# Grouped-query attention on one core: where VectorE computes the first step of its exponential correction, and when Q is transposed

## The chip, the core and the metric

The kernel runs on one core of a Trainium2 chip. Its engines are TensorE (PE in the profile; PEld is its weight load), VectorE (DVE), ScalarE (ACT), GpSimd (POOL) and SyncE (SP, which issues transfers here). The metric is the device time of one execution in microseconds (us); several executions are made and their median is compared.

## What is computed

```python
batch, seq, n_heads, n_kv_heads, dim = 8, 512, 32, 8, 64
K_expanded = np.repeat(K, heads_per_group, axis=2)      # heads_per_group = 4
V_expanded = np.repeat(V, heads_per_group, axis=2)
scores = np.einsum('bhqd,bhkd->bhqk', Q, K_expanded) * scale      # scale = 1/sqrt(dim)
weights = np.exp(scores - np.max(scores, axis=-1, keepdims=True))
weights = weights / (np.sum(weights, axis=-1, keepdims=True) + 1e-10)
output = np.einsum('bhqk,bhkd->bhqd', weights, V_expanded)
```

All inputs and the output are float32.

## The kernel before

The kernel takes the exponential without subtracting the maximum, and checks at the end whether the sums and V lay in bounds in which that is safe; if not, a second, general path computes everything again. Only the first path matters here.

The work is cut into 64 jobs. A job is one key/value head of one batch entry, with its four query heads. Two jobs make a unit `u` (a pair of key/value heads), so `u, g = divmod(j, 2)`. For each job TensorE computes the scores transposed (keys on the partitions, queries along the row), 16 blocks of 128 keys by 512 queries (four heads by four chunks of keys); each block is exponentiated into the tile `pt`; then TensorE multiplies `pt` with V, to which a column of ones is added, so that the product `pv` holds the outputs and the sums; VectorE takes the reciprocal of the sums (`inv`) and multiplies (`o_sb`), in two halves per job (`norm(j, 0)` and `norm(j, 1)`).

The exponentials are dealt to two routes:

- ScalarE does most: tiles of two blocks (128x1024, from an `s_ps` buffer, of which there are two) with an Exp activation (`act_tile`, L301). A job has seven of them, `act_tile(j, 0)` to `act_tile(j, 6)`.
- VectorE and GpSimd do the rest, `taken(j)` blocks of a job: two in a narrow job, three in a wide one. `WIDE(j)` holds for jobs from 4 on whose number isn't divisible by three, so a round of three jobs is narrow, wide, wide (called here the first and the second wide job). In a wide job `act_tile(j, 4)` is a half tile (128x512), which lies in one bank of `d_ps`.

The route of VectorE and GpSimd for the taken blocks has these steps: scores into `d_ps`; `u`, an affine map of the scores to 16-bit integers (VectorE, L312; two blocks at the job's start, and the third of a wide job already at the end of the job before); `f`, the low ten bits of u (VectorE, L323, the "and-step"); `g`, an affine map of f, the first step of the correction (GpSimd, L326); `w`, the product of g and f (GpSimd, L330); and `pt = u + w` (VectorE, L339, `exp_d4`, the "add"). The add of a job is done in the job after.

The products with V read the blocks of the upper half in the order 2, 3, 1, 0 of the key chunks, since VectorE's blocks lie in chunks 0 and 1; products from the 17th on need the add.

Q is loaded as it lies and transposed by TensorE against an identity, eight transposes a job (`trans_q`, L215) into one bank of `d_ps`, from which VectorE copies it to `qt` (L220). `d_ps` is one buffer of two banks, `pv` is one buffer of two banks, `s_ps` two buffers of two banks.

The order on each engine is the order in which the program issues its instructions, so each engine runs its own part of the loop body strictly in turn and waits where it needs another's result. In the middle of a job the order in the program is: the first half's normalization `norm(last, 0)`, tile 3, a new `d_ps` tile, tile 4 if the job is wide, the Q transposes of job j + 2, the check of sums (`check_sums`, L378, two VectorE instructions once in eight jobs, only in narrow jobs), the and-step, g and w of this job, the add of the last job, the copy of Q, tile 4 if the job is narrow, and then the products of the last job's second half, cut in three by `cut` with tiles 5 and 6 between, and the third block of the next job (`exp_d(j + 1, 2, ...)`) if that is wide.

The Tile layer adds the waits from what the instructions read and write. `apart` declares that two instructions don't depend on each other, where they touch different banks of one tile.

Of the kernel before, what the change touches and what calls it, by code (L numbers as in the profile page):

```python
# [40 lines left out]
WIDE = lambda j: j >= 4 and j % 3 > 0  # L41
# [26 lines left out]
def fast_path(ctx, tc, Q, K, V, out, flag, ident):  # L68
    nc = tc.nc
# [77 lines left out]
    def d_tile():  # L147
        return d_pool.tile([128, 2, S], FP32, name="d_ps")
# [3 lines left out]
    def first_k(gp, swap, bank):  # L152
        half_bank = bank.bitcast(BF16)[:, 0:S]
        ps = half_bank.rearrange("p (sc c) -> p sc c", sc=SC)
        h = 2 * gp
        done = []
        for sc in range(SC):
            if swap:
                for half, g in ((0, 1), (64, 0)):
                    done.append(nc.tensor.transpose(  # L160
                        ps[half:half + 64, sc, :], kn[0][:, sc, h + g, :], ident
                    ))
            else:
                done.append(nc.tensor.transpose(ps[:, sc, :], kn[0][:, sc, h:h + 2, :], ident))
        return done, lambda: nc.vector.tensor_copy(
            out=kt_first[:, gp, swap, :], in_=half_bank
        )
# [32 lines left out]
    def apart(this, other):  # L200
        if other is not None:
            tc.declare_no_dep(
                this.ins, other.ins, reason="the two are in different banks of one tile"
            )
        return this

    def trans_q(j, bank, lo=0, hi=NPAIR, other=None):
        u, g = divmod(j, 2)
        ps = bank.bitcast(BF16).rearrange("p (i sc c) -> p i sc c", i=NPAIR, sc=SC)
        done = []  # L210
        for i in range(lo, hi):
            for sc in range(SC):
                h = (u % 2) * 2 * HPG + g * HPG + 2 * i
                done.append(apart(
                    nc.tensor.transpose(ps[:, i, sc, :], qn[u // 2][:, sc, h:h + 2, :], ident),  # L215
                    other,
                ))
        if u not in qt:
            qt[u] = qt_pool.tile([128, 2, NPAIR, S], BF16, name="qt")
        return done, lambda: apart(nc.vector.tensor_copy(  # L220
            out=qt[u][:, g, lo:hi, :], in_=ps[:, lo:hi, :, :].rearrange("p i sc c -> p i (sc c)")
        ), other)
# [20 lines left out]
    NJOB = NU * 2  # L243
    DPAIR = NPAIR - 1

    def taken(j):
        return 1 if j == NJOB - 1 else 3 if WIDE(j) else 2

    def d_block(j):
        return SC * 2 - 2 if j == NJOB - 1 else 0  # L250

    def act_tiles(j):
        every = [(i, kc, m) for i in range(NPAIR) for kc in range(SC) for m in range(2)]
        first = DPAIR * SC * 2 + d_block(j)
        mine = [n for n in range(len(every)) if not first <= n < first + taken(j)]
        groups = [[n for n in mine if n // 2 == h] for h in range(len(every) // 2)]
        return [[every[n] for n in group] for group in groups if group]

    jobs, osb, invs = {}, {}, {}

    CHECKS = {}
    for b in range(B):
# [32 lines left out]
    def act_tile(j, n, spare=None):  # L295
        group = act_tiles(j)[n]
        i, kc, lo = group[0]
        ps = s_pool.tile([128, 2, S], FP32, name="s_ps") if spare is None else spare
        for _, _, m in group:
            scores(j, ps[:, m, :], i, kc, m)  # L300
        return nc.scalar.activation(  # L301
            out=jobs[j]["pt"][:, i, kc, lo:, :], in_=ps[:, lo:, :], func=EXP, scale=scale
        )

    def exp_d(j, lo, hi, ps, other=None):
        st = jobs.setdefault(j, {})
        if "u" not in st:
            for name, dtype in (("u", I16), ("f", I16), ("g", BF16), ("w", BF16)):
                st[name] = dve_pool.tile([128, 3, S], dtype, name=name + "16")[:, 0:taken(j), :]
        for n in range(lo, hi):  # L310
            apart(scores(j, ps[:, n - lo, :], DPAIR, *divmod(d_block(j) + n, 2)), other)
        return lambda: nc.vector.tensor_scalar(  # L312
            out=st["u"][:, lo:hi, :], in0=ps[:, 0:hi - lo, :], scalar1=A_U, scalar2=B_U,
            op0=ALU.mult, op1=ALU.add,
        )
# [3 lines left out]
    def exp_d2(j, engine=None):  # L319
        st = jobs[j]  # L320
        by_bits = engine is None
        engine = engine or nc.gpsimd
        nc.vector.tensor_single_scalar(  # L323
            out=st["f"], in_=st["u"], scalar=1023, op=ALU.bitwise_and
        )
        engine.tensor_scalar(  # L326
            out=st["g"], in0=st["f"], scalar1=-EXP_F1, scalar2=EXP_K * 2.0 ** (24 * by_bits),
            op0=ALU.add, op1=ALU.mult,
        )
        product = lambda: engine.tensor_tensor(  # L330
            out=st["w"], in0=st["g"], in1=st["f"].bitcast(FP16) if by_bits else st["f"],
            op=ALU.mult,
        )
        return product() if by_bits else product

    def exp_d4(j):
        st = jobs[j]
        n = taken(j)
        nc.vector.tensor_tensor(  # L339
            out=st["pt"][:, DPAIR, :, :, :].rearrange("p kc m q -> p (kc m) q")[  # L340
                :, d_block(j):d_block(j) + n, :
            ].bitcast(U16),
            in0=st["u"],
            in1=st["w"],
            op=ALU.add,
        )
# [8 lines left out]
    def pv(j, i, lo, hi):  # L355
        st = jobs[j]
        u, g = divmod(j, 2)
        b, gp = divmod(u, GP)
        if lo == 0:

            t = d_tile() if (j, i) == (NJOB - 1, 0) else pv_tile()
            t = t.rearrange("p m (qc c) -> p m qc c", qc=SC)
            st["pv"][i] = t[:, :, :, 0:D + 1]
        order = blocks(j, i)
        for n in range(lo, hi):
            kc, m, qc = order[n]
            nc.tensor.matmul(  # L367
                st["pv"][i][:, m, qc, :],
                st["pt"][:, i, kc, m, qc * 128:(qc + 1) * 128],
                vt[b % 2][:, kc, 2 * gp + g, :],  # L370
                start=(n < 2 * SC and qc == 0),
                stop=(n >= len(order) - 2 * SC and qc == SC - 1),
            )
# [139 lines left out]
    bank = pv_tile()  # L513
# [41 lines left out]
    bank = pv_tile()  # L555
# [7 lines left out]
    for j in range(1, NJOB - 1):  # L563
        last = j - 1
        u, g = divmod(j, 2)
        b, gp = divmod(u, GP)
        open_job(j)
        if j == 1:
            nc.gpsimd.tensor_copy(out=gate, in_=jobs[0]["pt"][0:1, 0, SC - 1, 0, 0:1])
        for load, *of in LOADS.get(j, ()):  # L570
            load(*of)
        if j == 1:
            dma_k(0, 2)
        if gp == 2 and g == 0 and b + 1 < B:
            dma_k(b + 1)

        cut = (11, 19) if taken(j) < 3 else (4, 18) if taken(last) < 3 else (4, 16)
        act_tile(j, 0)
        if j == 1:
            piece(1, *first_k(1, 0, bank[:, 1, S // 2:]))  # L580
        exp_d(j, 0, 2, d_tile())()
        act_tile(j, 1)
        if (j, 0) in CHECKS:
            check_v(*CHECKS[j, 0])
        pv(last, 0, 0, 16)
        act_tile(j, 2)
        pv(last, 0, 16, 32)
        norm(last, 0)
        act_tile(j, 3)

        reads = []
        bank = d_tile()
        beside = act_tile(j, 4, bank) if taken(j) > 2 else None

        ahead = (j + 1,) if j < 2 else (3, 4) if j == 2 else (j + 2,)
        for n, to in enumerate(ahead):
            if to < NJOB:
                reads.append(trans_q(to, bank[:, n, :], other=beside)[1])
        if j == 1:
            reads.append(first_k(1, 1, bank[:, 1, :])[1])  # L600
        if not WIDE(j):
            check_sums()
        exp_d2(j)
        exp_d4(last)
        copies = [read() for read in reads]
        if taken(j) == 2:
            act_tile(j, 4)
        pv(last, 1, 0, cut[0])
        act_tile(j, 5)
        if beside:  # L610
            pv(last, 1, *cut)
        if taken(j + 1) > 2:
            exp_d(j + 1, 2, taken(j + 1), bank[:, 1:2, :], copies[0])()
        if (j, 1) in CHECKS:
            check_v(*CHECKS[j, 1])
        if not beside:
            pv(last, 1, *cut)
        act_tile(j, 6)
        pv(last, 1, cut[1], 32)
        norm(last, 1)  # L620
        del jobs[last]

    j, last = NJOB - 1, NJOB - 2
# [144 lines left out]
```

## Time and profile before

| | |
|---|---|
| runs | 408.16, 408.46, 414.83 us; median 408.46 |
| profiled execution | 408.25 us; span of its instructions 406.5 us |
| mean granted TensorE clock | 0.999 |
| TensorE busy | 376.4 us, 93% of the span |
| VectorE busy | 353.0 us, 87% |
| ScalarE busy | 397.3 us, 98% |
| GpSimd busy | 328.2 us, 81% |
| g on GpSimd, 128x1536 | x40, mean 1971 ns |
| w on GpSimd, 128x1536 | x40, mean 3094 ns |
| Q copy on VectorE | x62, mean 682 ns |
| add on VectorE, 128x1536 | x40, mean 951 ns |

The table is read from the first and the fifth part of the page and from the groups by shape. Busy times are of the union of an engine's instructions, so where instructions of one engine overlap (ScalarE's do), the mean of one times their number is more than the busy time. A share of 100% isn't needed for an engine to set the time, and idle time of an engine that doesn't set it costs nothing. In rows of groups the columns are line, engine, operation, output and inputs with their shapes, count, busy time and mean ns of one, and idle time in front with what ended it. In rows of the timeline they are start, length, engine, line, operation, tiles, shapes, count of merged instructions and, in brackets, the idle time in front.

### The profile page before, as it was taken

What the parts mean: (1) busy time and instruction counts of PE and PEld (TensorE: products, weight loads), DVE (VectorE), ACT (ScalarE), POOL (GpSimd) and SP (SyncE); (2) the same over time, 40 slices, a digit from 0 to 9 for tenths busy, and PEclk for the clock granted to TensorE, in tenths of its full rate; (3) what the DMA queues carried; (4) which work ended last, traced back from release to release, by engine and by line L of the source; (5) the groups of instructions that cost most, each with busy time, mean ns of one, the idle gap of its engine ahead of it and who ended that gap; (6) DMA issues with size and microseconds to landing.
All of it is one profiled execution on the core that took longest, in us unless ns stands there. A gap on an engine that the chain in (4) does not pass through costs nothing.

```text
span 406.5 us, 12968 instructions
## 1 busy us (share of the span) xinstructions
PE 376.4 (93%) x5670; PEld 231.9 (57%) x5670; DVE 353.0 (87%) x618; ACT 397.3 (98%) x455; POOL 328.2 (81%) x181
## 2 busy tenths in 40 slices
PE   7999999999999999999999999999999999989985
PEld 3565565565555555655555555655565555655643
DVE  4788998988898989999889989889888999899875
ACT  5999999999999999999999999999999999999995
POOL 9978878878779879788888888788887798677682
PEclk9999999999999999999999999999999999999999
DMA  9999999977587996889497999949797496222205
GB/s 145 162 242 151 196 262 271 224 195 154 119 199 150 99 223 168 194 162 204 125 233 52 188 218 228 147 174 147 187 226 207 137 98 141 106 105 105 105 21 192
DMA packets 82892, 67.72 MB, mean 167 GB/s; under 512 B 52752, under 2 KB 57872, under 8 KB 82832
## 3 DMA queue, kind: packets, MB, share of 16 engines
q0 software_dynamic: 45072, 24.91, 52.0%
q1 hardware_dynamic: 37216, 41.75, 36.3%
q8 instruction: 45, 0.74, 0.8%
q10 hardware_dynamic: 544, 0.20, 0.2%
q14 instruction: 15, 0.12, 0.1%
HBM read 50.33 MB, written 33.55 MB: 206 GB/s over the span
## 4 chain that ended last, share of the span: by engine, by line
ACT 75%; PE 19%; DVE 3%; issue 1%; ACTq 0%; DVEq 0%
ACT pt L301 75%; PE s_ps L283 9%; PE pv L367 7%; PE d_ps L283 2%; DVE o_sb L414 1%; PE s_ps L503 1%; PE d_ps L215 1%; DVE u L312 0%; DVE pt L339 0%; ACT pt L535 0%; ACTq L301 0%; DVE inv_last L409 0%; PE d_ps L367 0%; DVE okv L238 0%; DVE ok L378 0%
## 5 line engine op out<-in xcount | busy, mean ns | idle before, releaser
L301 ACT ACTIVATE pt<-s_ps 128x1024 f16<-128x1024 f32 x408 | 385.7, 1179 | 0.5 <-PE s_ps L283 0.4
L367 PEld LDWEIGHTS <-pt 128*128 128x128 f16 x4096 | 142.6, 98 | 79.0 <-issue 50.5
L367 PE MATMUL pv<-v,pt 128*128 128x65 bf16 x4064 | 180.4, 195 | 2.3 <-DVE o_sb L414 1.2
L330 POOL TENSOR_TENSOR w<-g,f 128x1536 bf16<-128x1536 bf16 (+1 forms) x63 | 172.6, 2740 | 5.2
L283 PE MATMUL s_ps<-qt,kt 64*128 64x512 bf16 x761 | 152.8, 383 | 18.3 <-ACT pt L301 13.9
L326 POOL TENSOR_SCALAR g<-f 128x1536 bf16<-128x1536 int16 (+1 forms) x63 | 116.0, 1842 | 64.9 <-DVE f L323 64.8
L312 DVE TENSOR_SCALAR u<-d_ps 128x1024 int16<-128x1024 f32 (+1 forms) x104 | 104.5, 1004 | 0.3
L414 DVE TENSOR_TENSOR o_sb<-pv,inv 128x512 f32<-128x512 f32 x121 | 83.6, 691 | 4.2
L283 PEld LDWEIGHTS <-kt 64*128 64x128 bf16 x960 | 53.6, 93 | 58.8 <-issue 32.1
L409 DVE RECIPROCAL inv<-pv 128x8 f32<-128x8 f32 x121 | 25.1, 207 | 34.9 <-PE pv L367 33.8
L283 PE MATMUL d_ps<-qt,kt 64*128 64x512 bf16 x199 | 53.2, 375 | 1.5 <-DVE u L312 0.5
L339 DVE TENSOR_TENSOR pt<-u,w 128x1536 uint16<-128x1536 int16 (+1 forms) x64 | 54.2, 846 | 0.3 <-POOL w L330 0.2
L220 DVE COPY qt<-d_ps 128x1024 bf16<-128x1024 bf16 x62 | 42.2, 682 | 0.0
L215 PEld LDWEIGHTS <-q_nat 128*128 128x128 bf16 x508 | 28.5, 98 | 22.2 <-issue 22.2
L215 PE MATMUL d_ps<-ident,q_nat 128*128 128x128 bf16 x496 | 38.3, 220 | 0.0
L323 DVE TENSOR_SCALAR f<-u 128x1536 int16<-128x1536 int16 (+1 forms) x64 | 31.8, 498 | 0.0
L301 ACT ACTIVATE pt<-d_ps 128x512 f16<-128x512 f32 x40 | 30.4, 760 | 0.0
L238 DVE TENSOR_REDUCE okv<-v 128x1 f32<-128x512 bf16 x32 | 21.6, 675 | 0.0
L142 POOL DMA_DIRECT2D q_nat<-in_Q_dram x19 | 15.0, 791 | 0.1
L283 PE MATMUL s_ps<-qt,kt_first 64*128 64x512 bf16 x56 | 11.0, 395 | 1.9 <-ACT pt L301 1.5
L127 POOL DMA_DIRECT2D v<-in_V_dram x7 | 12.2, 1749 | 0.0
L283 PEld LDWEIGHTS <-kt_first 64*128 64x128 bf16 x64 | 4.0, 94 | 5.8 <-issue 3.2
(58 smaller groups left out, 50.8 us busy)
## 6 DMA issues: line engine op xcount, KB each, us to landing
out_dram<-o_sb SPq DMA_DIRECT2D x31, 1024.0 KB, 5.7
q_nat<-in_Q_dram POOLq DMA_DIRECT2D x14, 1024.0 KB, 12.3
k_nat<-in_K_dram POOLq DMA_DIRECT2D x7, 512.0 KB, 7.3
v<-in_V_dram POOLq DMA_DIRECT2D x7, 512.0 KB, 11.0
kt<-kt SPq DMA_DIRECT2D x14, 256.0 KB, 4.0
q_nat<-in_Q_dram POOLq DMA_DIRECT2D x3, 512.0 KB, 7.3
out_dram<-o_sb SPq DMA_DIRECT2D x4, 256.0 KB, 2.3
kt<-k_nat SPq DMA_TRANSPOSE x32, 6.0
```

The source lines that it names most:

```text
L215: nc.tensor.transpose(ps[:, i, sc, :], qn[u // 2][:, sc, h:h + 2, :], ident),
L220: return done, lambda: apart(nc.vector.tensor_copy(out=qt[u][:, g, lo:hi, :], in_=ps[:, lo:hi, :, :].rearrange("p i sc c -> p i (sc c)")), ...
L283: return nc.tensor.matmul(ps, keys[64 * m:64 * m + 64, g if u == 0 else g ^ m, kc * 128:(kc + 1) * 128], qt[u][64 * m:64 * m + 64, g, i, : ...
L301: return nc.scalar.activation(out=jobs[j]["pt"][:, i, kc, lo:, :], in_=ps[:, lo:, :], func=EXP, scale=scale)
L312: return lambda: nc.vector.tensor_scalar(out=st["u"][:, lo:hi, :], in0=ps[:, 0:hi - lo, :], scalar1=A_U, scalar2=B_U, op0=ALU.mult, op1=AL ...
L323: nc.vector.tensor_single_scalar(out=st["f"], in_=st["u"], scalar=1023, op=ALU.bitwise_and)
L326: engine.tensor_scalar(out=st["g"], in0=st["f"], scalar1=-EXP_F1, scalar2=EXP_K * 2.0 ** (24 * by_bits), op0=ALU.add, op1=ALU.mult,)
L330: product = lambda: engine.tensor_tensor(out=st["w"], in0=st["g"], in1=st["f"].bitcast(FP16) if by_bits else st["f"], op=ALU.mult,)
L339: nc.vector.tensor_tensor(out=st["pt"][:, DPAIR, :, :, :].rearrange("p kc m q -> p (kc m) q")[:, d_block(j):d_block(j) + n, :].bitcast(U16 ...
L367: nc.tensor.matmul(st["pv"][i][:, m, qc, :], st["pt"][:, i, kc, m, qc * 128:(qc + 1) * 128], vt[b % 2][:, kc, 2 * gp + g, :], start=(n < 2 ...
L409: nc.vector.reciprocal(out=inv, in_=sums[:, :, :, D:D + 1])
L414: nc.vector.tensor_tensor(out=osb[u][:, :, h:h + 2, :].rearrange("p qc m d -> p m qc d"), in0=sums[:, :, :, 0:D], in1=inv[:, :, :, None].t ...
```

## The change

In wide jobs the first step g moves from GpSimd to VectorE, right behind the and-step. The add of the last job moves ahead of the check of sums and the and-step. From job 3 on, the Q transposes are dealt differently: a narrow job transposes for jobs j + 2 and j + 3 (the second set into the second bank of `d_ps`, issued after tile 4), the first wide job for j + 3, the second wide job none. In narrow jobs the second half's products are cut at 4 and 19 instead of 11 and 19, and from job 3 on the middle part of them stands ahead of the next job's third block in narrow jobs too. The transposes are declared independent of the first copy, since they are in the other bank; the third block's scores are declared independent of the first copy only.

```diff
@@ trans_q
         if u not in qt:
             qt[u] = qt_pool.tile([128, 2, NPAIR, S], BF16, name="qt")
+        if other is not None and other.ins.engine == mybir.EngineType.DVE:
+            other = None
         return done, lambda: apart(nc.vector.tensor_copy(
@@ fast_path
+    def two_q(j):
+        return j > 2 and j % 3 == 0 and j + 3 < NJOB
@@ exp_d2
         by_bits = engine is None
+        first = nc.vector if engine or WIDE(j) else nc.gpsimd
         engine = engine or nc.gpsimd
         nc.vector.tensor_single_scalar(
             out=st["f"], in_=st["u"], scalar=1023, op=ALU.bitwise_and
         )
-        engine.tensor_scalar(
+        first.tensor_scalar(
             out=st["g"], in0=st["f"], scalar1=-EXP_F1, scalar2=EXP_K * 2.0 ** (24 * by_bits),
             op0=ALU.add, op1=ALU.mult,
         )
@@ the loop over jobs
-        cut = (11, 19) if taken(j) < 3 else (4, 18) if taken(last) < 3 else (4, 16)
+        cut = (4, 19) if two_q(j) else (11, 19) if taken(j) < 3 else (4, 18) if taken(last) < 3 else (4, 16)
...
-        ahead = (j + 1,) if j < 2 else (3, 4) if j == 2 else (j + 2,)
+        ahead = (j + 1,) if j < 2 else (3, 4) if j == 2 else ((j + 2,), (j + 3,), ())[j % 3]
...
+        exp_d4(last)
         if not WIDE(j):
             check_sums()
         exp_d2(j)
-        exp_d4(last)
         copies = [read() for read in reads]
         if taken(j) == 2:
             act_tile(j, 4)
+        if two_q(j):
+            copies.append(trans_q(j + 3, bank[:, 1, :], other=copies[0])[1]())
         pv(last, 1, 0, cut[0])
         act_tile(j, 5)
-        if beside:
+        if j > 2:
             pv(last, 1, *cut)
         if taken(j + 1) > 2:
-            exp_d(j + 1, 2, taken(j + 1), bank[:, 1:2, :], copies[0])()
+            exp_d(j + 1, 2, taken(j + 1), bank[:, 1:2, :], copies[0] if copies else None)()
         if (j, 1) in CHECKS:
             check_v(*CHECKS[j, 1])
-        if not beside:
+        if j < 3:
             pv(last, 1, *cut)
         act_tile(j, 6)
```

## The prediction

> **What bounds the kernel now.** I read the page's table of busy time first, then the groups, then ScalarE alone in the timeline, then one whole job in the timeline.
>
> ```profile
> PE 376.4 (93%) x5670; PEld 231.9 (57%) x5670; DVE 353.0 (87%) x618; ACT 397.3 (98%) x455; POOL 328.2 (81%) x181
> ...
> L301 ACT ACTIVATE pt<-s_ps 128x1024 f16<-128x1024 f32 x408 | 385.7, 1179 | 0.5 <-PE s_ps L283 0.4
> ```
>
> ScalarE is busy 98% of the span, and its main group waited 0.5 us in all. In the window from 6 to 402 us it is busy 394.90 of 396.00 us. A mean of 1179 ns times 408 would be 481 us, more than the 385.7 us of busy time, so its instructions overlap. What one really costs is seen in the timeline:
>
> ```profile
> 201.71 5.94 ACT L301 ACTIVATE pt<-s_ps 128x1024 f16<-128x1024 f32 x6
> 207.36 0.77 ACT L301 ACTIVATE pt<-d_ps 128x512 f16<-128x512 f32 x1
> 207.84 12.21 ACT L301 ACTIVATE pt<-s_ps 128x1024 f16<-128x1024 f32 x13
> ...
> 390.31 1.02 ACT L301 ACTIVATE pt<-s_ps 128x1024 f16<-128x1024 f32 x1 [0.20 <-PE s_ps L283]
> ```
>
> The columns are start, length, engine, line, operation, count. The thirteen tiles end at 220.05, the half tile before them at 208.13: 11.92/13 = 0.917 us a tile, with no loss inside. The last line is a tile that found ScalarE idle: 1.02 us. So a tile whose scores come late costs nothing as long as it starts 1.02 us before its due end (the end of the tile before, plus 0.917); later than that, all of it is lost. ScalarE's work (408 tiles of 0.917 and 40 half tiles of 0.48, 393 us) is untouched by the change, so the most it can win is the 1.1 us that ScalarE idles between 6 and 402.
>
> A narrow job (number divisible by three, two blocks on VectorE), here without the check of sums:
>
> ```profile
> 228.95 6.74 ACT L301 ACTIVATE pt<-s_ps 128x1024 f16<-128x1024 f32 x7
> 229.34 0.39 PE L283 MATMUL s_ps<-qt,kt 64*128 64x512 bf16 x2
> ...
> 229.66 0.67 PE L367 MATMUL pv<-v,pt 128*128 128x65 bf16 x16
> ...
> 230.37 0.21 DVE L409 RECIPROCAL inv<-pv 128x8 f32<-128x8 f32 x1 [0.33 <-PE pv L367]
> ...
> 230.61 0.69 DVE L414 TENSOR_TENSOR o_sb<-pv,inv 128x512 f32<-128x512 f32 x1
> ...
> 231.17 0.39 PE L283 MATMUL s_ps<-qt,kt 64*128 64x512 bf16 x2
> 231.22 0.42 DVE L323 TENSOR_SCALAR f<-u 128x1024 int16<-128x1024 int16 x1
> ...
> 231.55 0.95 DVE L339 TENSOR_TENSOR pt<-u,w 128x1536 uint16<-128x1536 int16 x1
> ...
> 232.30 0.37 PE L283 MATMUL d_ps<-qt,kt 64*128 64x512 bf16 x1
> ...
> 232.42 0.68 DVE L220 COPY qt<-d_ps 128x1024 bf16<-128x1024 bf16 x1
> ...
> 233.00 0.39 PE L283 MATMUL s_ps<-qt,kt 64*128 64x512 bf16 x2
> ```
>
> The scores at 229.34 are those of tile 2, at 231.17 of tile 4, at 232.30 the next job's third block, at 233.00 of tile 6, the job's last. Tile 6 is exponentiated from 233.47 to 234.78 and would have been in time if started by 233.76. Its scores ended at 233.39: the margin is 0.33 us. The third block's score, in front of it in TensorE's queue, waits for nobody here. A VectorE instruction that waits for nothing starts 0.085 us before the one ahead ends (231.64 against 231.55).
>
> **The change, part by part.** 1. The second VectorE copy. In 20 narrow jobs (3, 6, ... 60) two sets of Q transposes fill both banks of the d_ps tile, and the third block's score goes into the bank of the second set. It can then start only after the second copy, and tile 6's scores stand behind it in TensorE's queue. VectorE's queue from the normalization (ends 231.30) is now add, and-step, copy, copy. In times of the job shown: add 231.22 to 232.17, and-step 232.08 to 232.50, first copy 232.42 to 233.10, second 233.01 to 233.69. The second transposes (eight, 0.62 us) stand behind tile 4's scores and are over by 232.2, so only VectorE's queue decides. TensorE starts 0.06 us after the copy, at 233.75, tile 6's pair 0.01 later, done at 234.15; ScalarE starts at 234.19 and ends at 235.21 instead of 234.78: 0.43 us lost. Thirteen such jobs: 13 x 0.43 = 5.6 us.
>
> 2. The same where the check of sums falls in. It comes once in eight jobs and is done in the next narrow one: 9, 18, 27, 33, 42, 51, 57, so seven. Two instructions (0.61 us for both) now stand between add and and-step. In the job at 212.21 the normalization ends at 212.90; add from 212.82, check from 213.68, and-step 214.20, copies 214.54 and 215.13, the second ending at 215.82. Scores of tile 6 end at 216.28, ScalarE starts at 216.32 and ends at 217.34, against 216.38 before: 0.96 lost. 7 x 0.96 = 6.7 us.
>
> These two losses have no cover. The normalization waits for TensorE's 16 products, those for tile 2's scores, and those for ScalarE to free tile 0's buffer: tile 0 ends at 234.78 - 6 x 0.917 = 229.28, the scores start at 229.34. So VectorE can't be reached earlier.
>
> 3. The first step on VectorE in 40 wide jobs. The trace has it there only at 512 columns:
>
> ```profile
> L323 DVE TENSOR_SCALAR f<-u 128x1536 int16<-128x1536 int16 x40 | 22.0, 549 | 0.0
> ...
> L326 DVE TENSOR_SCALAR g<-f 128x512 bf16<-128x512 int16 x1 | 0.3, 294 | 0.0
> L323 DVE TENSOR_SCALAR f<-u 128x512 int16<-128x512 int16 x1 | 0.3, 289 | 0.0
> ```
>
> It takes 5 ns more than the and-step of its size, so at 1536 I take 0.555 us. The bound above is the row of u, 0.53 us per 512 columns beyond a fixed 0.16, so 1.74 us; nothing lets it be below 0.549. It must wait for the and-step's end (0.034 us, as between reciprocal and product), which also ends the 0.085 overlap: 0.555 - 0.085 + 0.12 = 0.59 us in VectorE's queue. In the second wide job it takes the place of a copy (0.60 net), so nothing moves. In the first wide job (normalization ends 200.91) the copy ends at 203.16 instead of 202.57, the third block's conversion at 203.77, the second normalization at 204.62 instead of 204.28, and TensorE's next products start at 204.69 instead of 204.35. The tile 2 behind them starts at 205.72 where 205.71 is the latest free start: 0.01 lost. The margin is used up, so I take 0.03 x 20 = 0.6 us, with 0 and 0.15 x 20 = 3 us as bounds.
>
> 4. GpSimd loses the step (40 x 1971 ns = 79 us) and is not on the path: its product ends before the add asks. In the second wide job it now starts at 227.30 and ends at 230.39, the add at 231.22. Its DMA issues and SP's keep their places; Q loads are issued more than three jobs ahead of use, so the earlier transposes find them landed. The same 62 sets of transposes and copies run.
>
> 5. The add ahead, and the later place of the products, are in the times above. In the last jobs VectorE also carries the closing sums; there the first step may lose up to 1 us, of which I take 0.
>
> Sum: 408.25 (the profiled execution; its span is 406.5) + 5.6 + 6.7 + 0.6 = 421.15, taken as 421. The median shown is 0.2 above that execution, well inside the uncertainty.
>
> By the Trainium skill, "ScalarE: Activation LUTs", section "What ACT_TABLE_LOAD costs", a lone tile would be 186 + 0.833 x 1024 = 1039 ns and back to back 93 less, an estimate of 946. The trace has 1020 and 917. By the page's figures each loss would be about the same, the sum within 0.5 us, but ScalarE's own work 12 us longer than was measured; the measurement decides.
>
> **Rivals.** A, not slower: the second wide job has no transposes any more (0.62 us of TensorE's time), so TensorE enters the narrow job with a lead, and the normalization comes early enough to hide the second copy. It decides from 0.43 us of lead (0.96 with the check); then 408.3 us. For it: TensorE is 93% busy and idles little. Against: tile 2's scores already start 0.06 us after their buffer is free, so a lead can't be used.
>
> B, half the loss: part of the queue is hidden, because with a later ScalarE the normalization comes 0.2 us earlier relative to it in every narrow job: 421 - 20 x 0.25 = 416. Against: the same 0.06 us.
>
> C, the loss goes on: after the late third score come its conversion (0.68), the second normalization and the next job's products, whose tile has about 0.2 us of margin; with the first wide job's used-up margin two more places lose 0.15 each per round: 421 + 20 x 0.3 = 427.
>
> D, the first step runs at u's rate: 1.18 us more in 40 jobs. In the first wide job all is lost, in the second about 0.8 after its margin: 421 + 20 x 2.0 = 461. Against: the 294 ns row.
>
> E, GpSimd's product comes late, since add, and-step and first step on VectorE hold it up, as its first step seems held now (1.04 us at its shortest, 1.68 typical at 1024 columns). The add in front then stops all of VectorE. It decides from 0.8 us of delay; at 1.0 us it costs 0.2 in each of 60 jobs: 433. Against: the product took 3.09 us in all 40 wide jobs. That the two engines block each other is a rule of the Trainium skill, "Advanced Engine Details and Errata", section "VectorE Performance Modes" (they share VectorE's second port); the 0.64 us on the first step is in line with it.
>
> **How the numbers follow.** Forecast 0.79, A 0.01, B 0.07, C 0.10, D 0.01, E 0.02. The predicted time is the forecast's, 421. The range reaches down to B's 416 and up to C's 427. A difference of 2% (8.2 us, so 400.1 or 416.6) is about what a measurement here can tell from none. Faster by that is excluded by the 1.1 us of ScalarE: 0.005. Within 2% are A, B and the lower edge of the forecast: 0.115. Slower: 0.88.
>
> **What would show it.** Right: ScalarE idle some 10 us in all, in 20 gaps of 0.3 and 0.85 us in front of a narrow job's last tile, released by TensorE; TensorE waiting for the copy (qt) at a d_ps score, 20 times; the first step on VectorE x40 at about 555 ns, VectorE near 375 us busy, GpSimd near 250. Wrong: no such gaps; the first step far from 0.55 us; VectorE waiting for w; or gaps spread over other tiles.

## The result, and the profile after

The changed kernel takes 426.33 us (median of six runs, 426.18 to 426.56), the kernel before 409.1 us in the same comparison (408.16 to 415.12). The ratio is 1.0433, with a 95% interval from 1.0415 to 1.045: slower. The forecast was 421, its range 416 to 427. The profiled execution took 426.18 us, against 408.25 before: 17.9 us more.

In the profiled executions of four experiments TensorE waits 1.8 to 4.3 us for a transfer of keys near 32 us, with a granted clock of 0.50 behind it, and other executions, some of the kernel before too, are longer without a trace that says why; so each experiment below is read by its shortest run beside the shortest of the kernel before (the ratios, with their intervals, are over several runs).

First the page and the waits of the changed kernel (L306 is the activation, L222 the copy of Q, L336 GpSimd's product):

```profile
PE 373.0 (88%) x5670; PEld 227.1 (54%) x5670; DVE 374.0 (88%) x658; ACT 401.2 (95%) x455; POOL 235.9 (56%) x141
...
DVE 58%; PE 28%; ACT 10%; issue 2%; ACTq 0%; DVEq 0%
...
L306 ACT ACTIVATE pt<-s_ps 128x1024 f16<-128x1024 f32 x408 | 383.8, 1061 | 14.7 <-PE s_ps L288 14.1
...
POOL w L336 <- DVE g L332: 133.9, 40, 5.2
PE d_ps L288 <- DVE qt L222: 16.4, 21, 1.2
ACT pt L306 <- PE s_ps L288: 14.1, 22, 1.1
```

ScalarE's group idled 0.5 us before and idles 14.7 now, 14.1 of it in 22 waits for scores (the wait rows give total, times and longest). TensorE waits 21 times for the copy of Q, 16.4 us in all. The chain that ended last was ScalarE for 75% before; now it is VectorE for 58%. VectorE's busy share hardly rose (87% to 88%): it is not full, it is late at one place.

That place, in a narrow job without the check of sums, in the timeline:

```profile
240.10 0.69 DVE L420 TENSOR_TENSOR o_sb<-pv,inv 128x512 f32<-128x512 f32 x1
240.71 0.95 DVE L345 TENSOR_TENSOR pt<-u,w 128x1536 uint16<-128x1536 int16 x1
...
241.57 0.42 DVE L329 TENSOR_SCALAR f<-u 128x1024 int16<-128x1024 int16 x1
...
241.91 1.28 DVE L222 COPY qt<-d_ps 128x1024 bf16<-128x1024 bf16 x2
...
243.24 0.37 PE L288 MATMUL d_ps<-qt,kt 64*128 64x512 bf16 x1 [0.63 <-DVE qt L222]
...
243.25 0.58 PE L288 MATMUL s_ps<-qt,kt 64*128 64x512 bf16 x2
...
238.61 4.74 ACT L306 ACTIVATE pt<-s_ps 128x1024 f16<-128x1024 f32 x5
243.88 1.94 ACT L306 ACTIVATE pt<-s_ps 128x1024 f16<-128x1024 f32 x2 [0.53 <-PE s_ps L288]
```

The normalization, the add, the and-step and both copies follow each other without idle time and end at 243.19. The third block's score waits 0.63 us for the second copy, and the last tile's pair of scores, queued behind it, takes 0.58 us. ScalarE has been done since 243.35. The late tile ends at 245.82 - 0.92 = 244.90; due was 243.35 + 0.92 = 244.27. The loss is 0.63 us.

Read in the same way at each place, twelve plain narrow jobs lose 0.61 to 0.63 us and the first one 0.34, and the seven with the check 1.14 to 1.17. VectorE's lateness in the first wide job, called "the first wide job's loss" below, shows at the third tile of the second wide job: 0.08 to 0.09 us in fifteen of the twenty rounds, and 0.23 in one more that loses nothing there in the kernel before. Together 7.5 + 0.3 + 8.1 + 1.3 + 0.2 = 17.4 of the 17.9 us; most of the rest is lost at the first tiles of three jobs, 0.13 to 0.26 us each. The same reading of the kernel before finds less than 1 us of loss between 20 and 400 us.

### The profile page after: what moved, and what is told of

Its sections match the earlier page's. It is cut to its first block, busy times and chain, and to the rows that moved or that the text cites. A ratio compares the mean times of both kernels' runs of the same rounds, so it can differ in the third digit from the quotient of the medians.

```text
span 424.3 us, 12967 instructions
## 1 busy us (share of the span) xinstructions
PE 373.0 (88%) x5670; PEld 227.1 (54%) x5670; DVE 374.0 (88%) x658; ACT 401.2 (95%) x455; POOL 235.9 (56%) x141
## 4 chain that ended last, share of the span: by engine, by line
DVE 58%; PE 28%; ACT 10%; issue 2%; ACTq 0%; DVEq 0%
DVE o_sb L420 16%; PE pv L373 16%; DVE u L317 10%; ACT pt L306 10%; PE s_ps L288 9%; DVE qt L222 8%; DVE pt L345 7%; DVE inv L415 4%; DVE okv L240 4%; DVE f L329 4%; DVE g L332 3%; PE d_ps L288 2%; DVE ok L384 1%; PE s_ps L509 1%; ACT pt L541 0%
## 5 line engine op out<-in xcount | busy, mean ns | idle before, releaser
L306 ACT ACTIVATE pt<-s_ps 128x1024 f16<-128x1024 f32 x408 | 383.8, 1061 | 14.7 <-PE s_ps L288 14.1
L336 POOL TENSOR_TENSOR w<-g,f 128x1536 bf16<-128x1536 bf16 (+1 forms) x63 | 172.5, 2738 | 135.9 <-DVE g L332 133.9
L288 PE MATMUL s_ps<-qt,kt 64*128 64x512 bf16 x761 | 156.2, 384 | 5.6 <-ACT pt L306 3.8
L288 PEld LDWEIGHTS <-kt 64*128 64x128 bf16 x960 | 49.3, 93 | 65.3 <-issue 43.5
L332 POOL TENSOR_SCALAR g<-f 128x1024 bf16<-128x1024 int16 x23 | 23.9, 1040 | 43.8 <-DVE f L329 43.7
L222 DVE COPY qt<-d_ps 128x1024 bf16<-128x1024 bf16 x62 | 40.6, 683 | 0.0
L306 ACT ACTIVATE pt<-d_ps 128x512 f16<-128x512 f32 x40 | 24.7, 616 | 0.0
L332 DVE TENSOR_SCALAR g<-f 128x1536 bf16<-128x1536 int16 (+1 forms) x41 | 22.7, 553 | 1.4
L288 PE MATMUL s_ps<-qt,kt_first 64*128 64x512 bf16 x56 | 10.9, 382 | 2.0 <-ACT pt L306 1.5
```

What stands on the lines that cost most here:

```text
L222: return done, lambda: apart(nc.vector.tensor_copy(out=qt[u][:, g, lo:hi, :], in_=ps[:, lo:hi, :, :].rearrange("p i sc c -> p i (sc c)")), ...
L288: return nc.tensor.matmul(ps, keys[64 * m:64 * m + 64, g if u == 0 else g ^ m, kc * 128:(kc + 1) * 128], qt[u][64 * m:64 * m + 64, g, i, : ...
L306: return nc.scalar.activation(out=jobs[j]["pt"][:, i, kc, lo:, :], in_=ps[:, lo:, :], func=EXP, scale=scale)
L332: first.tensor_scalar(out=st["g"], in0=st["f"], scalar1=-EXP_F1, scalar2=EXP_K * 2.0 ** (24 * by_bits), op0=ALU.add, op1=ALU.mult,)
L336: product = lambda: engine.tensor_tensor(out=st["w"], in0=st["g"], in1=st["f"].bitcast(FP16) if by_bits else st["f"], op=ALU.mult,)
```

## The experiments

The theory: the loss is the wait for the second copy of Q in narrow jobs, in front of the last tile's scores. Rival 1: VectorE's added work of 22 us is what is paid. Rival 2: two sets of transposes in one job hold up TensorE.

### The banks exchanged

```diff
-                reads.append(trans_q(to, bank[:, n, :], other=beside)[1])
+                reads.append(trans_q(to, bank[:, int(two_q(j)) if j > 2 else n, :], other=beside)[1])
...
-            copies.append(trans_q(j + 3, bank[:, 1, :], other=copies[0])[1]())
+            copies.append(trans_q(j + 3, bank[:, 0, :], other=copies[0])[1]())
...
-            exp_d(j + 1, 2, taken(j + 1), bank[:, 1:2, :], copies[0] if copies else None)()
+            exp_d(j + 1, 2, taken(j + 1), bank[:, 1:2, :], copies[-1] if copies else None)()
```

> The changed kernel with the two sets of Q transposes of a narrow job in exchanged banks: the first set goes into the bank that the next job's third block needs, the second set into the other. All work stays the same; the third block's score then waits for the first copy instead of the second, which ends 0.60 us earlier. Theory (the wait for the second copy, in front of tile 6): a plain narrow job loses 0.62 - 0.60 = 0.02 us, one with the check of sums 1.15 - 0.60 = 0.55 us, the first wide job its 0.09 as in the changed kernel: 7 x 0.55 + 13 x 0.02 + 20 x 0.09 = 5.9 us over 408.25, so 414 (412 to 415). Rival 1 (VectorE's added work of 22 us as such is paid for): nothing changes, 426. Rival 2 (two sets of transposes in one job hold up TensorE): nothing changes, 426.

Measured: 414.24 us (before beside it 407.81; ratio with its interval 1.0222, 1.0114 to 1.0329). The timeline of a plain narrow job:

```profile
236.29 0.68 DVE L222 COPY qt<-d_ps 128x1024 bf16<-128x1024 bf16 x1
236.43 0.37 PE L288 MATMUL d_ps<-qt,kt 64*128 64x512 bf16 x1
236.44 0.58 PE L288 MATMUL s_ps<-qt,kt 64*128 64x512 bf16 x2
236.01 2.98 ACT L306 ACTIVATE pt<-s_ps 128x1024 f16<-128x1024 f32 x3
```

The copy shown is the second; the score runs beside it, no longer behind it, and ScalarE goes from tile to tile without a gap. Plain narrow jobs lose 0.03 us at most, those with the check 0.54 to 0.57. By the shortest runs twelve us are gone with the same instructions on every engine, which neither rival allows.

### The third block behind the last tile

```diff
+        if two_q(j):
+            act_tile(j, 6)
         if taken(j + 1) > 2:
             exp_d(j + 1, 2, taken(j + 1), bank[:, 1:2, :], copies[0] if copies else None)()
...
-        act_tile(j, 6)
+        if not two_q(j):
+            act_tile(j, 6)
```

> The changed kernel with the scores of tile 6 issued ahead of the next job's third block in the narrow jobs; the third block still waits for the second copy, and the rest of the products stand behind it. Theory: tile 6 no longer waits, so the gap in front of it is gone, and so are the 0.19 us that the third block's score takes from tile 6's pair. What is late now is the third block, its conversion, the second normalization and with it the next job's products in front of its tile 2: about 0.2 us lost in a plain job, 0.7 with the check, and 0.1 to 0.2 in the first wide job: 13 x 0.2 + 7 x 0.7 + 20 x 0.15 = 10.5 over 408.25, so 419 (415 to 421). Rival 1 (VectorE's work): 426. If only tile 6's place mattered and nothing behind it: 410.

Measured: 423.24 us (1.0353, 1.0262 to 1.0444), above the expected range. The timeline shows where the wait went:

```profile
244.07 0.39 PE L288 MATMUL s_ps<-qt,kt 64*128 64x512 bf16 x2
244.77 0.37 PE L288 MATMUL d_ps<-qt,kt 64*128 64x512 bf16 x1 [0.30 <-DVE qt L222]
245.07 0.58 PE L373 MATMUL pv<-v,pt 128*128 128x65 bf16 x13
245.58 0.39 PE L288 MATMUL s_ps<-qt,kt 64*128 64x512 bf16 x2
...
246.06 1.94 ACT L306 ACTIVATE pt<-s_ps 128x1024 f16<-128x1024 f32 x2 [0.27 <-ACT pt L306]
```

The last tile's pair (244.07) is in time and takes 0.39 us, where behind the third score it took 0.58. But the third score still waits, and thirteen products and the next job's first tile (245.58) stand behind it. That tile is now late by 0.34 to 0.37 us (0.87 to 0.91 with the check), and the first wide job's loss is 0.20 to 0.23. I had looked for the next loss at that job's third tile, and had not priced the first. The wait was moved, not hidden.

### The first step and the add's place without the deal

```diff
     def two_q(j):
-        return j > 2 and j % 3 == 0 and j + 3 < NJOB
+        return False
...
-        ahead = (j + 1,) if j < 2 else (3, 4) if j == 2 else ((j + 2,), (j + 3,), ())[j % 3]
+        ahead = (j + 1,) if j < 2 else (3, 4) if j == 2 else (j + 2,)
```

> The first step on VectorE in wide jobs and the add ahead of the and-step, as in the changed kernel, but one set of Q transposes in every job (for job j + 2) and the old cuts: that is the change without its deal of the transposes. Theory: no second copy, so no loss in narrow jobs; left are the first wide job's 0.09 x 20 = 1.8 us and up to 1 us in the second wide job, which has its copy back: 410.5 (409 to 412). Rival 1 (VectorE's added work is paid for, 22 us): 426 or more, since VectorE has all of it. Rival 2 (the transposes): 408 to 410.

The middle products of narrow jobs keep their new place ahead of the third block too. Measured: 411.05 us, against 407.81 for the kernel before (1.0243, 1.0161 to 1.0324; the other runs took 417 to 421). VectorE carries all of its added work here, so rival 1 falls: what is left of the change is worth about 3 us of the 18.

The 3 us aren't where they were expected. The first wide job's loss is 0.00 in the rounds without a check and 0.23 to 0.26 in the seven with one, 1.7 us; a little more than 1 us is lost in the last jobs. That the time fell into the expected range is in part luck.

### The deal of the transposes alone

```diff
-        first = nc.vector if engine or WIDE(j) else nc.gpsimd
+        first = engine or nc.gpsimd
...
-        exp_d4(last)
         if not WIDE(j):
             check_sums()
         exp_d2(j)
+        exp_d4(last)
```

> The deal of the transposes and the cuts of the changed kernel, but the first step on GpSimd in all jobs and the add behind the and-step, as before the change. Theory: the second copy is there, so the narrow jobs lose what they lose in the changed kernel, 13 x 0.62 + 7 x 1.15 = 16.1 us, and the first wide job nothing: 424.3 (423 to 426). Rival 1 (VectorE's added work): 408 to 410.

Measured: 424.61 us (1.0432, 1.0349 to 1.0516). The narrow jobs lose 0.61 to 0.63 us and 1.14 to 1.16, as in the changed kernel; the 0.09 us of the first wide jobs are absent. So the deal alone, with its cuts and the products' new place, costs 16 us. The 0.09 us need both parts: they are absent here, where GpSimd does the first step, and absent without the deal in plain rounds, where VectorE does it.

### The check of sums behind the copies, alone and with the banks exchanged

```diff
-        if not WIDE(j):
+        if not WIDE(j) and not two_q(j):
             check_sums()
...
             copies.append(trans_q(j + 3, bank[:, 1, :], other=copies[0])[1]())
+            check_sums()
```

> The changed kernel with the check of sums (two VectorE instructions, in seven narrow jobs) issued behind the two copies instead of ahead of the and-step. Theory (VectorE's queue up to the second copy sets the loss): the seven jobs lose 0.62 like the others instead of 1.15, so 7 x 0.53 = 3.7 us less: 422.6 (421.5 to 424). In the trace the seven long gaps of about 1.05 us are gone and all are about 0.52 us. Rival (the seven jobs are longer for another reason, such as stores or loads that fall into them): 426.

> The changed kernel with the banks of a narrow job's two sets exchanged and the check of sums behind both copies: both parts of VectorE's queue that stand ahead of the third block's score without need are taken away. Theory: narrow jobs lose 0 to 0.05 us, with the check up to 0.15 by what it delays behind; left are the first wide job's 0.09 x 20 and the tail: 408.25 + 0.5 + 0.7 + 1.8 = 411.3 (410 to 413). That is no less than the kernel before, whose ScalarE idles 1.1 us in all. Rival (some cost of two sets of transposes in one job that the queue doesn't explain): 415 or more.

Measured: 439.79 and 431.95 us (1.071, 1.060 to 1.082; 1.0544, 1.0383 to 1.0704). The second run adds the exchange of the banks shown above. Both missed, by 17 and 21 us. The loss at the last tile fell as expected, to 0.61 to 0.64 us in the first kernel's seven jobs. What came instead is in its timeline (L384 is the check):

```profile
192.33 2.12 POOL L336 TENSOR_TENSOR w<-g,f 128x1024 bf16<-128x1024 bf16 x1
192.47 2.12 DVE L384 SCALAR_TENSOR_TENSOR ok<-inv,ok 128x128 f32<-128x128 f32 x1
...
194.52 0.68 DVE L317 TENSOR_SCALAR u<-d_ps 128x512 int16<-128x512 f32 x1
...
195.25 0.39 PE L288 MATMUL d_ps<-qt,kt 64*128 64x512 bf16 x2 [1.55 <-DVE u L317]
...
195.90 1.02 ACT L306 ACTIVATE pt<-s_ps 128x1024 f16<-128x1024 f32 x1 [1.03 <-PE s_ps L288]
```

The check's second instruction, 0.29 us elsewhere, took 2.12: it began while GpSimd's product ran, and ended 0.15 us after it. The third block's conversion stood behind it, and TensorE idled 1.55 us for that. The stretches of 1 us that follow (length, busy time and count of PE, PEld, DVE, ACT, POOL, then the granted clock, DMA share and GB/s):

```profile
194.00:195.00 1.00, 0.00 (x0) 0.00 (x0) 1.00 (x2) 0.87 (x1) 1.00 (x2) 1.00 0.52 109
...
197.00:198.00 1.00, 1.00 (x13) 0.59 (x12) 0.17 (x1) 0.47 (x1) 0.00 (x0) 0.50 0.98 62
```

Behind the idle stretch the granted clock is 0.50 for some 3 us, and ScalarE's next tiles come late too: 1.14 + 0.71 + 0.62 + 0.22 + 0.16 us in this job. In two of the seven places the clock stayed at 1.00; there the job lost 1.51 us, in the other five 2.85 to 3.35.

### The check of sums where GpSimd is idle

```diff
-        if not WIDE(j):
+        if j % 3 == 2:
             check_sums()
```

> The changed kernel with the check of sums moved from the narrow job to the second wide job, between the add and the and-step, where GpSimd has no instruction under way (its product waits for VectorE's first step there) and VectorE has no copy of Q. Theory: the seven narrow jobs lose 0.62 instead of 1.15; in the second wide job the check moves the second normalization by 0.5 us, of which 0 to 0.2 is lost: 426.3 - 7 x 0.53 + 7 x 0.15 = 423.7 (422 to 425), and each check instruction takes 0.28 to 0.29 us. Rival (the narrow jobs with the check lose more for another reason than VectorE's queue): 426 to 427.

Measured: 424.08 us (1.0375, 1.0306 to 1.0445). The row of the check's line in this kernel and, above it, in the one with the check behind the copies (shortest, median and longest in ns):

```profile
L384 DVE SCALAR_TENSOR_TENSOR ok<-inv,ok x16: 223/283/2125, 73.0 to 420.8; 128x128 f32<-128x128 f32 x14, 128x72 f32<-128x72 f32 x2
...
L384 DVE SCALAR_TENSOR_TENSOR ok<-inv,ok x16: 223/284/293, 81.1 to 401.3; 128x128 f32<-128x128 f32 x14, 128x72 f32<-128x72 f32 x2
```

So it is the meeting with GpSimd's product that lengthens the instruction. The narrow jobs right behind a check still lose 0.84 to 0.87 us, where 0.62 was expected, the others 0.61 to 0.63; seven jobs are 0.3 shorter than with the check inside, and the total fell by 2.1 us. With the banks exchanged as well:

> The changed kernel with the banks of a narrow job's two sets exchanged and the check of sums in the second wide job: nothing of VectorE's queue that the third block's score does without stands ahead of it. Theory: narrow jobs lose 0.02 us, first wide jobs 0.09, the check 0.1 to 0.2 in seven second wide jobs: 408.25 + 0.4 + 1.8 + 1 = 411.5 (410 to 413), about 15 us less than the changed kernel with the same instructions on every engine. Rival (two sets in one job, or the first step on VectorE, cost something apart from that wait): 415 or more.

Measured: 412.45 us, against 407.67 for the kernel before. Its profile shows at most 0.03 us lost in plain narrow jobs (0.10 in one), 0.24 to 0.28 in those behind a check, and 0.07 to 0.09 as the first wide job's loss. The same instructions as in the changed kernel, in another order and with two banks exchanged, take 14 us less. It doesn't beat the kernel before, and no order of the same ScalarE work could by more than the 1.1 us that ScalarE idles there.

### The first step back on GpSimd, the add still ahead

```diff
-        first = nc.vector if engine or WIDE(j) else nc.gpsimd
+        first = engine or nc.gpsimd
```

> The changed kernel with the first step of wide jobs back on GpSimd; the add stays ahead of the and-step. Theory: VectorE loses 22 us of work, but GpSimd's chain of a wide job (0.09 + 1.5 to 2.1 for the first step + 0.08 + 3.09 for the product) is 4.8 to 5.4 us, and from the and-step's end to the next job's add there are now 6.1 - 1.4 = 4.7 us. So the add waits for the product, 0.1 to 0.7 us in 40 jobs, with all of VectorE behind it, over the losses of the narrow jobs: 430 to 446, 436 taken. Rival (VectorE's added work is what costs): less than the changed kernel, 410 to 424.

Measured: 429.55 us (1.0444, 1.0341 to 1.0548), just below the expected range. The wait that I named is there, but only 16 times and not in 40 jobs:

```profile
DVE pt L345 <- POOL w L336: 4.1, 16, 1.0
```

Eleven plain narrow jobs lose 0.83 to 0.89 us where the changed kernel loses 0.62. That 22 us less work on VectorE makes the kernel 3 us slower is again against rival 1.

### The add behind the first step

```diff
-        exp_d4(last)
         if not WIDE(j):
             check_sums()
         exp_d2(j)
+        exp_d4(last)
```

> The changed kernel with the add of the last job behind the and-step and the first step, where it stood before the change. Theory: narrow jobs keep their losses (0.62 and 1.15). In wide jobs the add is 1.1 us later, and the products from the 17th on, which read what it writes, stand ahead of later tiles in TensorE's queue: 0.25 to 0.75 us lost per wide job on top: 424.4 + 20 x 0.5 = 434 (430 to 442). Rival (the add's place doesn't matter, as both orders have the same work): 426.

Measured: 437.60 us (1.0705, 1.0573 to 1.0837). TensorE's products wait for the add 21 times, 10.9 us in all:

```profile
PE pv L373 <- DVE pt L345: 10.9, 21, 0.6
```

ScalarE loses 0.41 to 0.44 us in one place more per round, and 0.13 more in the narrow jobs. So with the first step on VectorE, the add ahead of it is worth 11 us.

## Why the prediction was right, and where it fell short

- What bounds the kernel: right. ScalarE had nothing to win, and each late tile is lost in full beyond the 1.02 us rule: the losses read by that rule add up to 17.4 of the 17.9 us. The gaps are where they were foreseen, 0.50 to 0.53 and 1.03 to 1.06 us long instead of 0.3 and 0.85.
- Step 1, the second copy: the place and VectorE's queue were right. From the normalization's end to the second copy's end it is 240.79 to 243.19, 2.40 us; the prediction had 231.30 to 233.69, 2.39. The step that failed is "tile 6's pair 0.01 later, done at 234.15". It priced the pair at its usual 0.39 us; behind a single score it takes 0.58. That is 0.19 us in each of 20 jobs, 3.8 us. The trace of before has such a pair in every first wide job, and I didn't look at it:

```profile
202.20 0.37 PE L283 MATMUL d_ps<-qt,kt 64*128 64x512 bf16 x1
202.21 0.58 PE L283 MATMUL s_ps<-qt,kt 64*128 64x512 bf16 x2
```

- Step 2, the check: the same miss. Forecast 0.96, measured 1.14 to 1.17; the check's own part, 0.52 us, was right, as the difference to the plain jobs shows.
- Step 3, the first step on VectorE: 560 ns forecast as 555, and the queue behind it as forecast. What failed is its start: the sum took the first wide job's normalization as in the trace of before, where it ends 2.00 to 2.02 us after the job's first tile in rounds without a check. Behind a narrow job with two copies it ends 2.09 to 2.12 us after it, since the narrow job's second normalization, for which TensorE's products wait, comes 0.3 us later; in two rounds it ends after 2.00 to 2.01 us, and these lose nothing. The loss was 0.09 us and not 0.03, 0.9 us more in all, within the bounds that were given.

  The first row is of the kernel before, where the job's first tile ends at 198.90; the second of the changed kernel, where it ends at 245.82:

```profile
200.22 0.69 DVE L414 TENSOR_TENSOR o_sb<-pv,inv 128x512 f32<-128x512 f32 x1
...
247.21 0.69 DVE L420 TENSOR_TENSOR o_sb<-pv,inv 128x512 f32<-128x512 f32 x1
```

  The first miss and this one, 3.8 + 0.9, make up nearly all of the 5 us between 421 and 426. That 426 still lies inside the range is luck: its top of 427 was put there for rival C, and something else filled it.
- Step 4, GpSimd off the path: right, it now waits 133.9 us for the first step. It is busy 235.9 us and not the 250 forecast (the first row is of the kernel before):

```profile
L326 POOL TENSOR_SCALAR g<-f 128x1024 bf16<-128x1024 int16 x23 | 37.2, 1617 | 17.7 <-DVE f L323 17.6
...
L332 DVE TENSOR_SCALAR g<-f 128x1536 bf16<-128x1536 int16 x40 | 22.4, 560 | 1.4
...
L332 POOL TENSOR_SCALAR g<-f 128x1024 bf16<-128x1024 int16 x23 | 23.9, 1040 | 43.8 <-DVE f L329 43.7
```

  The first step of narrow jobs took 1617 ns in the mean before and takes 1040 now, since the add is over when it starts.
- Rival A (a lead of TensorE hides the copy): the normalization comes no earlier, as the queue shows. Rival B (half the loss) fell with the 0.63 us. Rival C (losses further on) has one place of the two that it named, with 0.09 us. Rival D fell with the 560 ns. Rival E, GpSimd and VectorE holding each other up, doesn't occur in the changed kernel, since its order keeps the two apart; it decides the two kernels with the check behind the copies, where it is VectorE that stands. The section of the Trainium skill that the prediction names there ("VectorE Performance Modes") speaks of VectorE's two-port instructions, and its table gives the add (tensor_tensor) no such mode.

## What to carry to other kernels

Where one engine is full, don't count another engine's added work but its latest result: 22 us more on VectorE, without the deal, cost 3 us, and one copy ahead of a score in a queue, at 20 places, cost 16 us. When two results share a buffer of two banks, give the bank that is asked for first to the copy that comes first; here that exchange alone was worth 12 us. Moving a waiting instruction back in its queue helps only if what is then behind it has room.

## What the runs showed of the hardware

- The check's second instruction (128x128, two inputs in SBUF) stood until GpSimd's product ended wherever it started during one: in the two kernels with the check behind the copies 14 of 14 took 2.12 to 2.13 us instead of 0.28 to 0.29, and ended 0.15 us after the product. The normalization, which reads one input from PSUM, took its 0.69 us during the product too. In the other order it is GpSimd that is held: its step took 1617 ns when it began during the add (two inputs in SBUF) and 1040 without. The Trainium skill says of it ("GPSIMD Engine Reference", section "Key points") that the two contend for SBUF interfaces when VectorE has two SBUF inputs; the trace agrees, and the VectorE instruction lost all that was left of the product.
- In the kernel with the check behind the copies TensorE idled 1.53 to 1.55 us at seven places, with 0.62 us of idling shortly before; at five of them the granted TensorE clock then went to 0.50 for about 3 us, at two it stayed at 1.00, as it did behind the changed kernel's seven stretches of 1.15 to 1.18 us. What decides between them is not shown. The Trainium skill ("TensorE: Matmul & The Clock Gate", section "Part 1: The HAM clock gate (the "warmup" mystery)") has the drop to half after an idle window of some 3.4 us; here shorter stretches were often enough.
- Scores over 64 rows run in pairs: two in 0.39 us, a single one and a pair behind it in 0.59 from the first's start.
